# Differential attention: four score maps of a head pair at once, and the long convolution's input made first

## The chip, the cores and the metric

The kernel runs on one core of one Trainium2 chip. The metric is the time of one execution on the device in microseconds (us); three runs of the kernel before gave a median of 2513.32 us. Every number of the trace comes from one profiled execution.

## What is computed

Two transformer blocks stand one behind the other. The first has an mLSTM layer and a latent-attention (MLA) layer, each with a convolutional feed-forward part. The second block has two layers (l = 0, 1), each with four token mixers side by side and an MLP. 256 latent tokens and 256 context tokens run through both; in layer 1 of the second block only the latent tokens are needed at the end. The change is in the second block's mixers, of which two matter here, cut to what is computed:

```python
DIFF_HEADS, DIFF_DQK, CONV_A_K, GROUP_W = 4, 32, 31, 256

def diff_attention(q1, q2, k1, k2, v, lam, lam_init, subln_g):
    scale = DIFF_DQK ** -0.5
    ...
        p1 = jax.nn.softmax(jnp.einsum('bqhd,bkhd->bhqk', qb1, k1).astype(jnp.float32) * scale, axis=-1)
        p2 = jax.nn.softmax(jnp.einsum('bqhd,bkhd->bhqk', qb2, k2).astype(jnp.float32) * scale, axis=-1)
        w = (p1 - lam * p2).astype(v.dtype)
        return jnp.einsum('bhqk,bkhd->bqhd', w, v)
    ...
    o = rms_norm(o, subln_g) * (1.0 - lam_init)

def conformer_conv(a_val, a_gate, conv_w, conv_b, ln_g, ln_b):
    glu = a_val * jax.nn.sigmoid(a_gate)
    y = depthwise_conv(glu, conv_w) + conv_b
    return jax.nn.silu(layer_norm(y, ln_g, ln_b))

    # token_mixers: four mixers, put together and projected
    return jnp.concatenate([y_a, y_b, y_c, y_d], axis=-1) @ w_out
```

So a head has two score maps, each over a contraction of only 32, and the convolution runs over 31 taps of a gated projection. The other two mixers are a spatial gating and a short convolution of 3 taps.

## The kernel before

**Arithmetic.** Every product is made of three matmuls (high x high, high x low, low x high; `mm3`, lines 284 to 286), of operands that `split` (L263, L264) or `weight` (L278, L279) has taken apart: ScalarE rounds the high part, VectorE subtracts it. Weights come in pieces of 512 KB into `raw`.

**Banks.** PSUM has eight banks: four of the pool `pm` (projections and transposes, `mm_ps`), three of `px` (scores, sums, rotations, `ax_ps`), one of `pa`. A tile whose pool is full waits until the oldest tile's readers are done.

**Order.** The kernel is written as one program; a scheduler then sets each engine's order within the limits of data and buffers. What is written earlier goes earlier where both are ready, and `high_priority` lifts the transposes and the weighted values of an item. Each engine runs its own queue in order, so an instruction that waits holds all that stand behind it on that engine.

**The mLSTM's values.** `values_of` (L804) opens four tiles, one for each 128 of a head's 512 value columns, and adds up 16 blocks of the input into each of them. Close to it a head's normalisation runs: sums over tokens by a matmul with ones (L310), eight small steps on VectorE (L845, and L320 to L326, an inverse square root) and a broadcast back by TensorE (L334). The first layer's start (L610 and on) opens seven tiles at once, four `pm` and three `px`.

**The mixers.** `_mixers` (L1363) prepares keys, queries and values, and then runs a loop over the score items. In layer 0 there are two groups, the context (256 queries, 256 keys) and the latent tokens (256 queries, 512 keys); in layer 1 only the latter. A unit is a pair of tiles j, a group and a head g; with two query halves qt that gives 16 items in layer 0 and 8 in layer 1. `probs` makes the two maps of one head in two `px` banks: three matmuls of 32 rows for each, the two strips of 32 rows alternating (L1601), a maximum over each (L1604, VectorE), its negation (L1605), an exponential with its sum (L1608, ScalarE), a reciprocal and a product with 1 and minus lambda (L1611, L1612), and the difference of the two maps (L1613 on ScalarE, L1614 on VectorE). `mix` transposes the result (L1192, `pm`), splits it and multiplies it with the values; `subln` is the head norm (L1650, L1658, L1661).

**The fill.** Beside each item the loop steps a generator `fill`, by the table FS, which makes the remaining projections. In layer 0 it goes: keys and queries of the latent tokens (four pieces), their values, then `gated` (two pieces), then gating and the short convolution, and then the parts of the output projection (`w_oa`). In layer 1 keys, queries and values are made ahead of the loop, so `gated` is the first of the fill. `gated` (L1390) makes the input of the long convolution: two projections, a memset of the tile with its margins (GpSimd), a sigmoid and a product. Once both are there, the loop steps `taps` (L1435), two taps at a time on VectorE (L1444), four such steps per item in layer 0 and three in layer 1. When the taps are through, `conv_norm` follows, with tiles of `px`; what is left of the taps follows behind the loop. The maps of two items stay in the queue (`finish(2)`).

## Time and profile before

| what | value |
|---|---|
| runs | 2507.35, 2513.32, 2513.51 us |
| profiled execution | 2507.25 us |
| its span, first to last instruction | 2505.5 us |
| TensorE busy | 2407.6 us (96%) |
| VectorE busy | 1619.3 us (65%) |
| ScalarE busy | 1109.9 us (44%) |
| mean granted clock of TensorE | 0.976 of full |
| mixers of layer 0 / of layer 1 | about 1558 to 1722 / 2189 to 2290 us |

The names are read so: `px<-a,a 32*128 32x512` is a matmul that writes a tile of `px` from two `a` tiles, with 32 rows of weights, and 512 columns that move. "xcount" joins equal instructions that follow each other; the duration then is that of all of them. The time of a matmul is modelled at its end, so the distance from start to start is the better price. Shares of busy time are means over stages with different limits; the stretches are of more use than the page's totals.

### The profile page before, as it was taken

What the parts mean: (1) busy time and instruction counts of PE and PEld (TensorE: products, weight loads), DVE (VectorE), ACT (ScalarE), POOL (GpSimd) and SP (SyncE); (2) the same over time, 40 slices, a digit from 0 to 9 for tenths busy, and PEclk for the clock granted to TensorE, in tenths of its full rate; (3) what the DMA queues carried; (4) which work ended last, traced back from release to release, by engine and by line L of the source; (5) the groups of instructions that cost most, each with busy time, mean ns of one, the idle gap of its engine ahead of it and who ended that gap; (6) DMA issues with size and microseconds to landing.
All of it is one profiled execution on the core that took longest, in us unless ns stands there. A gap on an engine that the chain in (4) does not pass through costs nothing.

```text
span 2505.5 us, 36625 instructions
## 1 busy us (share of the span) xinstructions
PE 2407.6 (96%) x14362; PEld 2076.6 (83%) x14362; DVE 1619.3 (65%) x2953; ACT 1109.9 (44%) x1879; POOL 11.4 (0%) x20
## 2 busy tenths in 40 slices
PE   7998999999998999999999999989899999998998
PEld 5876888788897878878887999867888888977998
DVE  3867444544567756557676677797865556697665
ACT  4743333422445423235545456554523324465543
POOL 0000000000000000000000000000000000000000
PEclk9999999999999999999998999998899999998999
DMA  8676223433324554556337554222445455233553
GB/s 300 198 233 221 86 85 112 132 93 118 108 78 143 162 158 160 180 165 206 128 119 253 192 179 150 72 84 81 137 157 175 146 160 185 64 91 104 188 183 119
DMA packets 114750, 369.72 MB, mean 148 GB/s; under 512 B 12688, under 2 KB 17040, under 8 KB 114576
## 3 DMA queue, kind: packets, MB, share of 16 engines
q1 hardware_dynamic: 114576, 367.37, 45.0%
q8 instruction: 113, 1.85, 0.3%
q14 instruction: 61, 0.50, 0.1%
HBM read 357.88 MB, written 9.44 MB: 147 GB/s over the span
## 4 chain that ended last, share of the span: by engine, by line
PE 86%; DVE 5%; DMA 3%; ACT 3%; issue 2%; SPq 0%; DVEq 0%; ACTq 0%
PE pm L284 23%; PE pm L285 23%; PE pm L286 22%; PE px L284 4%; PE px L285 4%; PE px L286 4%; DMA raw<-in_ada 2%; DVE a L451 1%; PE px L1601 1%; PE pa L410 1%; PE px L310 1%; DVE wl L279 1%; PE pm L1192 1%; PE px L334 1%; DVE a L279 1%
## 5 line engine op out<-in xcount | busy, mean ns | idle before, releaser
L284 PE MATMUL pm<-a,wh 128*128 128x512 f32 (+1 forms) x2432 | 839.7, 347 | 6.6 <-DVE a L264 3.3
L286 PE MATMUL pm<-a,wl 128*128 128x512 f32 (+1 forms) x2432 | 834.5, 344 | 2.6 <-DVE wl L279 2.6
L285 PE MATMUL pm<-a,wh 128*128 128x512 f32 (+1 forms) x2432 | 836.9, 345 | 0.0
L278 ACT CAST wh<-raw 128x1024 fp32r<-128x1024 f32 (+2 forms) x421 | 420.1, 1002 | 800.1 <-PE pm L285 443.3
L279 DVE TENSOR_TENSOR wl<-raw,wh 128x1024 fp32r<-128x1024 f32 (+2 forms) x421 | 488.2, 1162 | 312.8 <-ACT wh L278 310.5
L284 PEld LDWEIGHTS pm<-a,wh 128*128 128x128 f32 x2432 | 463.3, 191 | 79.7 <-ACT wh L278 11.5
L286 PEld LDWEIGHTS pm<-a,wl 128*128 128x128 f32 x2432 | 463.8, 191 | 56.6 <-DVE wl L279 3.7
L285 PEld LDWEIGHTS pm<-a,wh 128*128 128x128 f32 x2432 | 464.8, 191 | 53.0 <-issue 1.6
L451 DVE SCALAR_TENSOR_TENSOR a<-raw,cs,a 128x1024 f32<-128x1024 f32 x168 | 211.0, 1281 | 91.3 <-DMA raw<-in_ada 89.2
L284 PE MATMUL pm<-a,a 128*128 128x256 f32 (+2 forms) x844 | 245.2, 303 | 16.9 <-ACT a L278 7.6
L285 PE MATMUL pm<-a,a 128*128 128x256 f32 (+2 forms) x844 | 248.8, 297 | 1.5 <-DVE a L279 0.9
L286 PE MATMUL pm<-a,a 128*128 128x256 f32 (+2 forms) x844 | 246.4, 295 | 0.4 <-DVE a L279 0.4
L284 PEld LDWEIGHTS pm<-a,a 128*128 128x128 f32 x844 | 162.8, 197 | 29.1 <-ACT a L278 10.1
L285 PEld LDWEIGHTS pm<-a,a 128*128 128x128 f32 x844 | 166.4, 197 | 4.4 <-DVE a L264 1.2
L286 PEld LDWEIGHTS pm<-a,a 128*128 128x128 f32 x844 | 165.8, 197 | 2.7 <-DVE a L279 0.6
L530 DVE SCALAR_TENSOR_TENSOR a<-pm,mod,a 128x256 f32<-128x256 f32 x188 | 87.3, 480 | 69.5 <-PE pm L286 68.6
L284 PE MATMUL pm<-wh,a 128*128 128x512 f32 (+1 forms) x336 | 128.1, 384 | 3.3 <-ACT a L263 3.3
L285 PE MATMUL pm<-wl,a 128*128 128x512 f32 (+1 forms) x336 | 129.3, 385 | 0.0
L263 ACT CAST a<-t 128x256 fp32r<-128x256 f32 (+2 forms) x173 | 86.1, 505 | 95.4 <-DVE t L1741 49.2
L286 PE MATMUL pm<-wh,a 128*128 128x512 f32 (+1 forms) x336 | 126.0, 383 | 0.0
L284 PE MATMUL px<-a,wh 128*128 128x256 f32 (+1 forms) x364 | 120.3, 331 | 0.0
L285 PE MATMUL px<-a,wh 128*128 128x256 f32 (+1 forms) x364 | 119.7, 330 | 0.0
(309 smaller groups left out, 2940.8 us busy)
## 6 DMA issues: line engine op xcount, KB each, us to landing
raw<-in_ada SPq DMA_DIRECT2D x192, 512.0 KB, 4.3
raw<-in_w_m SPq DMA_DIRECT2D x128, 512.0 KB, 4.2
raw<-in_ffn_in SPq DMA_DIRECT2D x88, 512.0 KB, 4.1
raw<-in_w_qk SPq DMA_DIRECT2D x32, 512.0 KB, 3.6
raw<-in_w_v SPq DMA_DIRECT2D x32, 512.0 KB, 3.5
raw<-in_ffn_oa SPq DMA_DIRECT2D x32, 512.0 KB, 3.6
raw<-in_w_inb SPq DMA_DIRECT2D x28, 512.0 KB, 3.5
raw<-in_w_up SPq DMA_DIRECT2D x16, 512.0 KB, 4.7
```

The costliest lines, as they stand in the source:

```text
L263: self.nc.scalar.copy(hi, src)
L278: nc.scalar.copy(hi, raw)
L279: nc.vector.tensor_sub(lo, raw, hi.bitcast(F32))
L284: mm(out, ah, bh, start=start, stop=False)
L285: mm(out, ah, bl, start=False, stop=False)
L286: mm(out, al, bh, start=False, stop=stop)
L310: self.nc.tensor.matmul(out_ps[:, i * nt + t:i * nt + t + 1], a[:, c0 + t * P:c0 + (t + 1) * P], self.ones[:, 0:1], start=(k == 0), stop=( ...
L334: self.nc.tensor.transpose(ps[:, t * P:(t + 1) * P], col[:, t:t + 1].to_broadcast([P, P]), self.ident)
L410: nc.tensor.matmul(ps[32 * j:32 * j + 32, 0:256], self.cs[:, l // 2, kt, :], raw[:, j, :], start=(kt == 0), stop=(kt == KD - 1), tile_posi ...
L451: nc.vector.scalar_tensor_tensor(s, raw, c, s, op0=ALU.mult, op1=ALU.add)
L530: self.nc.vector.scalar_tensor_tensor(z[:, a:b], ps[:, a:b], gate[:, kt, w:w + 1], z[:, a:b], op0=ALU.mult, op1=ALU.add)
L1192: nc.tensor.transpose(pt[:, s * P:(s + 1) * P], p[:, s * P:(s + 1) * P], K.ident)
```

## The change

- The pools: `pm` has three banks instead of four, `px` four instead of three. Where four or seven tiles are open at once (`values_of`, the mLSTM's start), the fourth of `pm` becomes one of `px`.
- `probs` makes all four maps of a pair of heads in one item: twelve matmuls on the four strips of 32 rows, in turns, into four `px` banks. An item is now a pair of heads and a query half: 8 items in layer 0 and 4 in layer 1. One reciprocal and one product with lambda serve all four maps; two of the four exponentials go to a tile of the pool `a`. `mix` transposes for both heads and opens the `pa` tile just ahead of the products with the values.
- In `fill`, `gated` stands first in both layers.
- The steps per item are set anew (FS; taps by five steps per item in layer 0 and eight in layer 1, the last one being that of the check `next`), and one item stays in the queue instead of two.

```diff
@@ -189,8 +189,8 @@
-        self.pm = E(tc.tile_pool(name="pm", bufs=4, space=bass.MemoryType.PSUM))
-        self.px = E(tc.tile_pool(name="px", bufs=3, space=bass.MemoryType.PSUM))
+        self.pm = E(tc.tile_pool(name="pm", bufs=3, space=bass.MemoryType.PSUM))
+        self.px = E(tc.tile_pool(name="px", bufs=4, space=bass.MemoryType.PSUM))
@@ -610,7 +610,7 @@
-    pss = [K.mm_ps() if f < 4 else K.ax_ps() for f in range(NU)]
+    pss = [K.mm_ps() if f < 3 else K.ax_ps() for f in range(NU)]
@@ -802,7 +802,7 @@
     def values_of(hd):
-        vps = [K.mm_ps() for _ in range(4)]
+        vps = [K.mm_ps() for _ in range(3)] + [K.ax_ps()]
@@ -1557,6 +1557,9 @@
     def fill():
+        for f in range(2):
+            gated(f)
+            yield
         if l == 0:
             for f in range(2):
                 qk_of(kp[f], wk[f], TC, T)
@@ -1565,9 +1568,6 @@
             v_of(vw(), HALVES[1])
-            yield
-        for f in range(2):
-            gated(f)
             yield
@@ -1585,58 +1585,64 @@
-    units = [(j, q0, ns, g) for q0, ns in groups for j in range(2) for g in range(2)]
-
-    def probs(j, q0, ns, g, qt):
+    items = [(j, q0, ns, qt) for q0, ns in groups for j in range(2) for qt in range(2)]
+
+    def probs(j, q0, ns, qt):
...
-        st = K.sp.tile([P, 3, 2], F32, name=K.uid("sd"), tag="sd", bufs=4)
-        p = []
-        ps = [K.ax_ps() for _ in range(2)]
-
-        for n, (u, w) in enumerate(((0, 0), (0, 1), (1, 0))):
-            for i in range(2):
-                rows = slice(64 * g + 32 * i, 64 * g + 32 * i + 32)
-                nc.tensor.matmul(ps[i][:, 0:nk], qp[j][rows, u, sl], kp[j][rows, w, 0:nk],
-                                 start=(n == 0), stop=(n == 2))
-        for i in range(2):
+        st = K.sp.tile([P, 3, 4], F32, name=K.uid("sd"), tag="sd", bufs=4)
+        w = K.a4()
+        ps = [K.ax_ps() for _ in range(4)]
+
+        for n, (u, v) in enumerate(((0, 0), (0, 1), (1, 0))):
+            for i in range(4):
+                rows = slice(32 * i, 32 * i + 32)
+                nc.tensor.matmul(ps[i][:, 0:nk], qp[j][rows, u, sl], kp[j][rows, v, 0:nk],
+                                 start=(n == 0), stop=(n == 2), tile_position=(32 * i, 0))
+        for i in range(4):
             nc.vector.tensor_reduce(st[:, 0, i:i + 1], ps[i][:, 0:nk], axis=AX.X, op=ALU.max)
-        nc.vector.tensor_scalar(st[:, 0], st[:, 0], -scale, None, op0=ALU.mult)
-        for i in range(2):
-            t = K.t2()
-            nc.scalar.activation(t[:, 0:nk], ps[i][:, 0:nk], AF.Exp, bias=st[:, 0, i:i + 1], scale=scale,
+            if i % 2 == 1:
+                nc.vector.tensor_scalar(st[:, 0, i - 1:i + 1], st[:, 0, i - 1:i + 1], -scale, None, op0=ALU.mult)
+        t = []
+        for i in range(4):
+            t.append(w[:, i // 2] if i % 2 == 0 else K.t2())
+            nc.scalar.activation(t[i][:, 0:nk], ps[i][:, 0:nk], AF.Exp, bias=st[:, 0, i:i + 1], scale=scale,
                                  accum_out=st[:, 1, i:i + 1])
-            p.append(t)
         nc.vector.reciprocal(st[:, 2], st[:, 1])
-        nc.vector.tensor_mul(st[:, 2], st[:, 2], lam2)
-        nc.scalar.activation(p[0][:, 0:nk], p[0][:, 0:nk], AF.Copy, scale=st[:, 2, 0:1])
-        nc.vector.scalar_tensor_tensor(p[0][:, 0:nk], p[1][:, 0:nk], st[:, 2, 1:2], p[0][:, 0:nk],
-                                       op0=ALU.mult, op1=ALU.add)
-        return p[0]
+        nc.vector.tensor_tensor(st[:, 2].rearrange("p (g i) -> p g i", g=2), st[:, 2].rearrange("p (g i) -> p g i", g=2),
+                                lam2.unsqueeze(1).to_broadcast([P, 2, 2]), op=ALU.mult)
+        for g in range(2):
+            x = w[:, g, 0:nk]
+            nc.scalar.activation(x, x, AF.Copy, scale=st[:, 2, 2 * g:2 * g + 1])
+            nc.vector.scalar_tensor_tensor(x, t[2 * g + 1][:, 0:nk], st[:, 2, 2 * g + 1:2 * g + 2], x,
+                                           op0=ALU.mult, op1=ALU.add)
+        return w
...
-    FS = ([1] * 8 + [1, 2] * 4, [1] * 4 + [2] * 4)
+    FS = ([2] * 4 + [3] * 4, [2] * 2 + [4] * 2)
     for i, u in enumerate(items):
         queue.append((u, probs(*u)))
         step(filler, FS[l][i])
         if len(glu) == 2 and conv is not None:
-            step(conv, (3,2)[l])
+            step(conv, (4, 7)[l])
...
-        finish(2)
+        finish(1)
```

TensorE, layer 0, the first item of the latent tokens: scores (L1601 before, L1602 now), projections (L284 to L286), the head norm's broadcast (L1661, L1667). Before, a head's two maps of one query half and, 22 rows on, its first map of the other half:

```order
L1661 MATMUL px2328_14623<-cst_89,sq2329_14624 128x128 x2
L1601 MATMUL px2333_14644<-a2189_13789,a2191_13791 128x512
L1601 MATMUL px2334_14645<-a2189_13789,a2191_13791 128x512
L1601 MATMUL px2333_14644<-a2189_13789,a2191_13791 128x512
L1601 MATMUL px2334_14645<-a2189_13789,a2191_13791 128x512
L1601 MATMUL px2333_14644<-a2189_13789,a2191_13791 128x512
L1601 MATMUL px2334_14645<-a2189_13789,a2191_13791 128x512
L285 MATMUL pm2355_14743<-wl2365_14784,a2049_12934 128x512
L286 MATMUL pm2355_14743<-wh2364_14783,a2049_12934 128x512
...
L286 MATMUL pm2356_14744<-wh2367_14801,a2058_12955 128x512
L1601 MATMUL px2344_14713<-a2189_13789,a2191_13791 128x512 x3
L284 MATMUL pa2314_14554<-a2341_14706,a2220_13970 128x256
```

Now:

```order
L1667 MATMUL px2354_14803<-cst_89,sq2355_14804 128x128 x2
L1602 MATMUL px2363_14839<-a2189_13789,a2191_13791 128x512
L1602 MATMUL px2364_14840<-a2189_13789,a2191_13791 128x512
L1602 MATMUL px2363_14839<-a2189_13789,a2191_13791 128x512
L1602 MATMUL px2364_14840<-a2189_13789,a2191_13791 128x512
L1602 MATMUL px2363_14839<-a2189_13789,a2191_13791 128x512
L1602 MATMUL px2364_14840<-a2189_13789,a2191_13791 128x512
L1602 MATMUL px2365_14841<-a2189_13789,a2191_13791 128x512 x3
L284 MATMUL pm2340_14719<-wh2343_14723,a2037_12906 128x512
...
L284 MATMUL pm2341_14720<-wh2346_14741,a2043_12920 128x512
L1602 MATMUL px2366_14842<-a2189_13789,a2191_13791 128x512 x3
L285 MATMUL pm2340_14719<-wl2347_14742,a2043_12920 128x512
```

Three of the four maps are in one piece, the third behind the first two; the fourth stands 15 rows on. Before, the second item's two maps were in separate places too.

TensorE, the mLSTM: values of one head (`pm`, and the fourth tile), sums L310 and broadcast L334. Before:

```order
L285 MATMUL pm624_3899<-wl634_3964,a527_3354 128x512
L310 MATMUL px618_3873<-hm_91,az606_3798 128x1 x4
L286 MATMUL pm624_3899<-wh633_3963,a527_3354 128x512
L284 MATMUL pm625_3900<-wh633_3963,a527_3354 128x512
...
L286 MATMUL pm624_3899<-wh636_3993,a531_3364 128x512
L284 MATMUL pm625_3900<-wh636_3993,a531_3364 128x512
L334 MATMUL px621_3888<-cst_89,rs620_3880 128x128 x4
L285 MATMUL pm625_3900<-wl637_3994,a531_3364 128x512
```

Now:

```order
L284 MATMUL pm624_3899<-wh633_3963,a527_3354 128x512
L285 MATMUL pm624_3899<-wl634_3964,a527_3354 128x512
L286 MATMUL pm624_3899<-wh633_3963,a527_3354 128x512
L310 MATMUL px618_3873<-hm_91,az606_3798 128x1 x4
L334 MATMUL px621_3888<-cst_89,rs620_3880 128x128 x4
L284 MATMUL px625_3900<-wh627_3903,a517_3329 128x512
L285 MATMUL px625_3900<-wl628_3904,a517_3329 128x512
```

The broadcast came 26 rows behind the sums and is now right behind them; the fourth tile's 18 matmuls on the same weights follow it. The same stands in three heads; in the fourth the two are apart as before.

VectorE, layer 0, the first taps (L1442, L1444) with the product that makes their input (L1400), maxima (L1604 before, L1605 now) and weight splits (L279). Before:

```order
L1611 RECIPROCAL sd2278_14343<-sd2278_14343 128x2 [waits Activation_49]
L1612 TENSOR_TENSOR sd2278_14343<-sd2278_14343,lt0_13776 128x2 [waits DVE_49]
L1400 TENSOR_TENSOR a2291_14425<-t2292_14427,pm2283_14363 128x2x256 [waits Activation_49,Pool_49]
L1614 SCALAR_TENSOR_TENSOR t2281_14355<-t2282_14357,sd2278_14343,t2281_14355 128x256 [waits Activation_49]
L1442 TENSOR_SCALAR a2310_14530<-a2291_14425,pv_87 128x512 [waits DVE_49]
L1444 SCALAR_TENSOR_TENSOR a2310_14530<-a2291_14425,pv_87,a2310_14530 128x512 [waits DVE_49] x2
L1604 TENSOR_REDUCE sd2295_14443<-px2297_14445 128x1 [waits PE_49]
L1444 SCALAR_TENSOR_TENSOR a2310_14530<-a2291_14425,pv_87,a2310_14530 128x512 [waits DVE_49]
```

Now:

```order
L279 TENSOR_TENSOR wl2247_14144<-raw2245_14141,wh2246_14143 128x1024 [waits DMAHW2_49,PE_49,Activation_49]
L1400 TENSOR_TENSOR a2238_14104<-t2239_14106,pm2230_14042 128x2x256 [waits PE_49,Activation_49,Pool_49]
L279 TENSOR_TENSOR wl2301_14496<-raw2299_14493,wh2300_14495 128x1024 [waits DMAHW3_49,Activation_49]
L1442 TENSOR_SCALAR a2250_14176<-a2238_14104,pv_87 128x512 [waits DVE_49]
L1444 SCALAR_TENSOR_TENSOR a2250_14176<-a2238_14104,pv_87,a2250_14176 128x512 [waits DVE_49] x5
L279 TENSOR_TENSOR wl2304_14502<-raw2302_14499,wh2303_14501 128x1024 [waits DMAHW4_49,PE_49,Activation_49]
L1444 SCALAR_TENSOR_TENSOR a2250_14176<-a2238_14104,pv_87,a2250_14176 128x512 [waits DVE_49] x4
L1400 TENSOR_TENSOR a2248_14171<-t2249_14173,pm2240_14109 128x2x256 [waits PE_49,Activation_49,Pool_49]
L1605 TENSOR_REDUCE sd2251_14188<-px2255_14192 128x1 [waits PE_49]
L1605 TENSOR_REDUCE sd2251_14188<-px2256_14193 128x1 [waits PE_49]
```

The taps began ahead of the second maximum of the seventh of 16 items, and now begin between the maxima of the second of eight.

## Rows read from the trace of the kernel before

**Rows 1.** The page: busy time by engine; the last chain by line.

```profile
PE 2407.6 (96%) x14362; PEld 2076.6 (83%) x14362; DVE 1619.3 (65%) x2953; ACT 1109.9 (44%) x1879; POOL 11.4 (0%) x20
...
PE pm L284 23%; PE pm L285 23%; PE pm L286 22%; PE px L284 4%; PE px L285 4%; PE px L286 4%; DMA raw<-in_ada 2%; DVE a L451 1%; PE px L1601 1%; PE pa L410 1%; PE px L310 1%; DVE wl L279 1%; PE pm L1192 1%; PE px L334 1%; DVE a L279 1%
```

**Rows 2.** Busy time by stretch, columns as in the first line.

```profile
core 0: us, PE busy (x) PEld busy (x) DVE busy (x) ACT busy (x) POOL busy (x), PEclk, DMA share, GB/s
1558.00:1612.00 54.00, 53.90 (x346) 46.06 (x346) 39.02 (x104) 36.89 (x88) 1.09 (x2) 1.00 0.20 64
1612.00:1710.00 98.00, 89.63 (x417) 70.49 (x416) 92.81 (x206) 47.61 (x88) 0.00 (x0) 0.91 0.22 68
2189.00:2257.00 68.00, 60.10 (x375) 49.88 (x373) 63.62 (x159) 42.70 (x80) 0.00 (x0) 0.93 0.30 90
2257.00:2290.00 33.00, 28.79 (x198) 27.93 (x199) 26.36 (x78) 14.16 (x28) 0.00 (x0) 0.78 0.24 64
1657.00:1663.70 6.70, 6.66 (x19) 5.23 (x20) 6.43 (x18) 3.21 (x8) 0.00 (x0) 0.50 0.15 42
2247.30:2271.20 23.90, 15.10 (x63) 13.24 (x63) 21.51 (x77) 7.41 (x17) 0.00 (x0) 0.50 0.09 23
```

**Rows 3.** TensorE's waits, layer 0 (two lines) and layer 1.

```profile
PE px L1601 <- ACT t L1608: 7.2, 3, 4.6
PE pm L284 <- DVE a L264: 2.6, 1, 2.6
...
PE px L1661 <- DVE sq L1658: 6.5, 2, 6.0
```

**Rows 4.** VectorE's groups, 1558 to 1722: count, busy us, mean ns, idle.

```profile
L1444 DVE SCALAR_TENSOR_TENSOR a<-a,pv,a 128x512 f32<-128x512 f32 x60 | 44.3, 745 | 0.1
L279 DVE TENSOR_TENSOR wl<-raw,wh 128x1024 fp32r<-128x1024 f32 x19 | 23.1, 1219 | 1.0 <-ACT wh L278 1.0
L1604 DVE TENSOR_REDUCE sd<-px 128x1 f32<-128x512 f32 x16 | 10.7, 684 | 1.7 <-PE px L1601 1.7
...
L1611 DVE RECIPROCAL sd<-sd 128x2 f32<-128x2 f32 x16 | 2.6, 162 | 6.6 <-ACT t L1608 6.6
```

**Rows 5.** VectorE's timeline, the first taps: start us, us, instruction, xcount.

```profile
1604.11 1.54 DVE L1444 SCALAR_TENSOR_TENSOR a<-a,pv,a 128x512 f32<-128x512 f32 x2
```

**Rows 6.** TensorE's timeline at two groups of scores; columns as above.

```profile
1630.94 0.96 PE L1601 MATMUL px<-a,a 32*128 32x512 f32 x6
1631.83 0.50 PE L285 MATMUL pm<-wl,a 128*128 128x512 f32 x1
1632.17 0.40 PE L286 MATMUL pm<-wh,a 128*128 128x512 f32 x1
1632.40 0.40 PE L285 MATMUL pm<-wl,a 128*128 128x512 f32 x1
...
1637.07 0.96 PE L1601 MATMUL px<-a,a 32*128 32x512 f32 x3
1637.96 0.39 PE L284 MATMUL pa<-a,a 128*128 128x256 f32 x1
```

**Rows 7.** ScalarE's groups in 1558 to 1722.

```profile
L1608 ACT ACTIVATE t<-px,sd 128x512 f32<-128x512 f32 x16 | 10.8, 684 | 1.6 <-DVE sd L1605 1.5
L1608 ACT ACT_TABLE_LOAD x6 | 7.7, 1283 | 0.1
...
L1608 ACT ACTIVATION_READ_ACCUMULATOR t<-px,sd 128x1 f32 x32 | 6.3, 198 | 0.0
```

**Rows 8.** Timeline of TensorE and VectorE at one mLSTM head's sums.

```profile
568.41 0.95 PE L310 MATMUL px<-hm,az 128*128 128x1 f32 x8
569.22 0.49 PE L286 MATMUL pm<-wh,a 128*128 128x512 f32 x1
...
570.59 0.17 DVE L326 SCALAR_TENSOR_TENSOR rs<-rs 128x4 f32<-128x4 f32 x1
```

**Rows 9.** TensorE's waits in 1030 to 1300, the MLA part.

```profile
PE pm L284 <- DVE a L264: 0.7, 1, 0.7
```

More of the change, by code (lines that the diff above doesn't have):

```diff
@@ L1609, in probs @@
                                  accum_out=st[:, 1, i:i + 1])
-            p.append(t)
         nc.vector.reciprocal(st[:, 2], st[:, 1])
-        nc.vector.tensor_mul(st[:, 2], st[:, 2], lam2)
-        nc.scalar.activation(p[0][:, 0:nk], p[0][:, 0:nk], AF.Copy, scale=st[:, 2, 0:1])
-        nc.vector.scalar_tensor_tensor(p[0][:, 0:nk], p[1][:, 0:nk], st[:, 2, 1:2], p[0][:, 0:nk],
-                                       op0=ALU.mult, op1=ALU.add)
-        return p[0]
-    pso, hl = [None], [None]
@@ L1620, in mix @@
-    def mix(j, q0, ns, g, qt, p):
-        if g == 0 and qt == 0:
-            pso[0] = K.pa.tile([P, 512], F32, name=K.uid("pa"), tag="pa")
-        if qt == 0:
-            if ns == 2:
-                t = K.a4(F32R, (P, 4, TC))
-                hl[0] = t[:, 0:2], t[:, 2:4]
-            else:
-                hl[0] = K.a4(F32R, (P, 4, TC)), K.a4(F32R, (P, 4, TC))
-        hi, lo = hl[0]
-        _transposed(K, p, ns, hi, lo, qt * P)
+        nc.vector.tensor_tensor(st[:, 2].rearrange("p (g i) -> p g i", g=2), st[:, 2].rearrange("p (g i) -> p g i", g=2),
+                                lam2.unsqueeze(1).to_broadcast([P, 2, 2]), op=ALU.mult)
@@ new lines, in probs, with mix @@
+        for g in range(2):
[4 more added lines that the diff above has]
+        return w
+    pso, hl = [None], [None, None]
+    def mix(j, q0, ns, qt, w):
+        if qt == 0:
+            for g in range(2):
+                if ns == 2:
+                    t = K.a4(F32R, (P, 4, TC))
+                    hl[g] = t[:, 0:2], t[:, 2:4]
+                else:
+                    hl[g] = K.a4(F32R, (P, 4, TC)), K.a4(F32R, (P, 4, TC))
+        for g in range(2):
+            _transposed(K, w[:, g], ns, *hl[g], qt * P)
@@ L1631, in mix @@
         if qt == 0:
             return
-        for s in range(ns):
-            K.mm3(pso[0][:, q0:q0 + TC], vz[s][:, 0, 2 * j + g, :], vz[s][:, 1, 2 * j + g, :],
-                  hi[:, s], lo[:, s], g == 0 and s == 0, g == 1 and s == ns - 1)
-        if g == 1:
-            if len(yb) <= j:
-                yb.append(K.a4())
-            nc.scalar.copy(yb[j][:, 0, q0:q0 + TC], pso[0][:, q0:q0 + TC])
+        pso[0] = K.pa.tile([P, 512], F32, name=K.uid("pa"), tag="pa")
+        for g in range(2):
+            hi, lo = hl[g]
+            for s in range(ns):
+                K.mm3(pso[0][:, q0:q0 + TC], vz[s][:, 0, 2 * j + g, :], vz[s][:, 1, 2 * j + g, :],
+                      hi[:, s], lo[:, s], g == 0 and s == 0, g == 1 and s == ns - 1)
@@ L1641, in _mixers @@
+        if len(yb) <= j:
+            yb.append(K.a4())
+        nc.scalar.copy(yb[j][:, 0, q0:q0 + TC], pso[0][:, q0:q0 + TC])
     ybp = {}
@@ L1691, in conv_norm @@
         yield
-    items = [u + (qt,) for u in units for qt in range(2)]
     queue, tails = [], []
@@ L1698, in finish @@
         while len(queue) > n:
-            u, p = queue.pop(0)
+            u, w = queue.pop(0)
             with K.tc.high_priority(60):
-                mix(*u, p)
-            if u[3:] == (1, 1) and u[:2] != (1, TC):
+                mix(*u, w)
+            if u[3] == 1 and u[:2] != (1, TC):
                 tails.append(subln(*u[:2]))
-    FS = ([1] * 8 + [1, 2] * 4, [1] * 4 + [2] * 4)
+    FS = ([2] * 4 + [3] * 4, [2] * 2 + [4] * 2)
     for i, u in enumerate(items):
```

## Prediction

> **What bounds the kernel now.** I read the page first, then the busy time by stretch, then the waits, then single matmuls. The page says that the kernel as a whole is bound by TensorE: 96% of the span; the score matmuls (line L1601) are 1% of the chain that ended last [rows 1]. A change to the score maps can therefore only win where these stages are not held by TensorE alone. There are two such stages, both in the second block: the mixers of layer 0 (1558 to 1722 us) and of layer 1 (2189 to 2290 us). The stretches [rows 2] show a turn inside layer 0. Until 1612 TensorE has no free time (53.90 of 54 us) and VectorE has 15 us of it (39.02 of 54). From 1612 to 1710 it is VectorE that is full (92.81 of 98 us), while TensorE is idle for 8.4 us and its mean clock drops to 0.91. Layer 1 is alike: VectorE 63.62 of 68 us up to 2257, then TensorE at a mean clock of 0.78. The waits [rows 3] name three stalls: scores that wait for the exponentials of an earlier unit (7.2 us, longest 4.6), a projection that waits for a split (2.6), and in layer 1 the sums of squares behind VectorE (6.5, longest 6.0). Inside the stretches after such stalls the granted clock is 0.50, the lower of the two levels (1.2 GHz) [rows 2].
>
> VectorE is full from 1612 on because of the long convolution: 60 taps of 745 ns, 44.3 us, in layer 0 alone [rows 4]. The first of them starts at 1604.11 [rows 5], 46 us into the stage, since its input (`gated`) is made in layer 0 only after five other pieces of the fill.
>
> **The change part by part.**
>
> *Scores on four strips.* Six matmuls on two strips, alternating, take 1630.94 to 1631.83 = 0.89 us; three on a single strip take 1637.07 to 1637.96 = 0.89 too [rows 6]. So two strips already run wholly side by side, and a group costs what three matmuls in a row cost. Two units in one group would save 0.89 us, and some 0.2 us for entering and leaving the group (the matmul behind one, at 1631.83, stands 0.34 us from the next, where 0.23 is usual [rows 6]; I take as much on the other side). But the order of the instructions does not put the four strips together. Of the four latent items of layer 0 none has its twelve matmuls in one piece; they stand as ten groups, where eleven were. In layer 1 two items of four stand whole and one nearly so: seven groups, where twelve were. That is 6 x 1.09 = 6.5 us of TensorE less. The context's maps, of half the columns, go from 10 groups to 12; at half of 0.89 and the same 0.2 that is 1.3 us more. Net 5 us of TensorE, and all but the context's part lies where VectorE, not TensorE, sets the end. I count nothing for it by itself; the bounds are 0 and -5.
>
> The Trainium skill, "TensorEngine Tiling (Array Packing)", Key Properties, says that a change of tiling mode drains TensorE. The trace agrees in size: about 0.1 us on either side [rows 6]. The Trainium skill, "TensorE: Matmul & The Clock Gate", Measured speedup vs the span model, gives 3.07x for four row tiles; by that a full group of four would take some 1.16 us instead of 0.89, an estimate, and as few such groups exist the sum would move by under 1 us.
>
> *Smaller things on VectorE and ScalarE.* Reciprocal and the multiply by lambda go from 24 to 12 each. At 162 ns, the reciprocal's time [rows 4], layer 0 saves 8 + 8 of them, 2.6 us of VectorE; layer 1 saves 4 + 4, 1.3 us. Exponentials stand closer together: three table loads fewer at their line, of 1283 ns each [rows 7], on ScalarE, which is not full (36.89 of 54 us at its most in layer 0 [rows 2]). Nothing counted.
>
> *The convolution's input first, layer 0.* By the order of TensorE, `gated` now stands right behind the first scores, ahead of the other projections. Counted in matmuls at their spacing of before, the first half is there near 1574 instead of just ahead of 1604 [rows 5], and the taps start during the second of the eight items. Between 1574 and 1604 VectorE's free share is 1 - 39.02/54 = 0.28 [rows 2], so 30 x 0.28 = 8 us of taps move out of the full stretch. With the 2.6 us above VectorE has 10.6 us less to do after 1612. VectorE is the bound there, so the stage ends about that much sooner. What is late next is TensorE: it has 89.6 busy us in the 98 from 1612 on, part of it at half clock, so it follows a VectorE that is 10 us sooner if fewer stalls also give back clock. Bounds: as little as 2 us (only the removed operations count, the taps merely push other things on VectorE's queue, weight splits L279 and transposed splits L264, into the early stretch where TensorE is the bound); as much as 17 us (TensorE's whole loss from 1612 to 1710: 8.4 us idle, and 0.09 x 98 = 8.8 us by the clock [rows 2], of which [rows 2] has one piece). I take -10, near the row that bounds it from VectorE's free time.
>
> *Layer 1.* `gated` was first there already, so only the rates change: eight double taps per item instead of three. The taps end with the fourth item and the normalisation follows inside the loop. The stall of 6.0 us before the sums of squares [rows 3] comes from VectorE's queue, where a small chain stands between taps. In the new order some taps still stand there. Saved: 1.3 us of small operations and about half of that stall, 4 us together; bounds 0 and 12 (all of TensorE's free time in both stretches). I take -4.
>
> *One bank from `pm` to `px`.* All of the kernel has three `pm` banks now. In the mLSTM the values of a head need four; the fourth is now `px`. The scheduler then puts 18 of its matmuls behind the others. With that, the sums L310 and the broadcast L334 are adjacent on TensorE in three heads; before, 26 rows of values stood between them. The chain between the two is in the trace: the next matmul after the sums starts at 569.22, and VectorE's eight steps end at 570.59 + 0.17 = 570.76 [rows 8]. So 1.5 us were hidden behind matmuls and stand open now, plus about 0.1 to start: 3 x 1.6 = +4.8 us. Bounds: +3 (a little overlap of the weight loads) and +8.4, if each time a weight split of 1219 ns [rows 4] stands ahead of the chain on VectorE. [...] In the MLA part the transposes share three banks where four were; TensorE waits there for a split only 0.7 us in all [rows 9]; I take +1, bounds 0 and +3. In the ffn and the mlp a tile of `pm` is open for several us of matmuls while its reader takes under 1 us, so the third bank hides that; if that cover fails, about 0.5 us per pair.
>
> *Sum*: -10 - 4 + 4.8 + 1 = -8.2 us. The profiled execution took 2507.25 us, span and 1.75 us around it, so 2499.0. The three runs lie at 2507.35, 2513.32 and 2513.51; the profiled one is at their lower end, and the same step from the median gives 2505.1. I state 2502, between the two.
>
> **The rivals.**
>
> *A: it cancels.* The bank taken from `pm` costs 8 + 3 us and layer 0 gives 6, layer 1 gives 3: +2, about 2509 to 2513. For it: what opens in the mLSTM is certain by the order, and the gain rests on VectorE's free time. Against it: VectorE is full in both places, and the taps do move.
>
> *B: slower, all four banks in one item.* An item takes all of `px`, and the next one's first map waits for the first map's maximum and exponential: 684 ns [rows 4] + 162 for the negation + 684 + 198 to read the sum [rows 7], 1.7 us. Other users of `px` (sums of squares, rotations, the short convolution) have to be let in between. If each of 12 items shows that, 12 x 1.7 = 20 us come on top: -8.2 + 20 = +12, 2519 from the profiled run and up to 2525 from the median. It decides from the point where the fill between two items is shorter than that chain plus what stands ahead of it on VectorE. For it: L1601 waits for exponentials already, with three banks and two taken at a time [rows 3]. Against it: there is fill between items, and a wait of TensorE costs nothing while VectorE is the bound.
>
> *C: it does not do what it says.* The four strips are mostly apart in the order, so the part that gives the change its name yields the 0 that I count; if in addition `gated` only swaps places with other full work, what is left is the removed small operations against the mLSTM's stalls: -3.9 + 5.8 = +2, 2509. For it: the order. Against it: the free 15 us of VectorE ahead of 1612.
>
> *D: layer 0 comes free.* With taps started 30 us sooner VectorE is no longer the bound, the three stalls go, the clock stays at its upper level: -17 - 8 + 5.8 = -19, 2488 to 2494. [...] Against it: 92.81 us of VectorE work do not shrink by more than 10.
>
> **How the numbers follow.** Forecast 0.42, A 0.20, B 0.17, C 0.09, D 0.12. 0.3% (7.5 us) is about what a measurement of this kernel can tell from no change. The forecast lies close to that bound: of its 0.42 I give 0.32 to faster and 0.10 to the same. D is faster. A and C are mostly the same (0.21), with 0.06 slower and 0.02 faster. B is slower. Together faster 0.46, same 0.31, slower 0.23. The range reaches up into B (2520) and takes in the bank's upper bounds with little gain (2507 + 8.4 + 3), and down past D by the rest of layer 1's bound and the scores' 5 us: 2483 to 2520.
>
> **What would show it.** Right: the first tap about 25 us after the stage's start instead of 46, VectorE's share before 1612 up from 39 of 54, the stage of layer 0 about 10 us shorter, L310 to L334 with 1.5 us of TensorE idle in three heads. Rival B shows as a larger wait of the score line for the exponentials; D as a mean clock near 1.0 in layer 0. Wrong: if the taps start early and the stage is no shorter, VectorE was not its bound; if the mLSTM has no new stall, the trace hid a row that the order has.

## The result

The changed kernel takes 2529.61 us (median of four runs, 2523.62 to 2531.24) against 2511.06 for the kernel before: ratio 1.0073, 95% interval 1.0051 to 1.0096. It is slower by about 18 us, where 8 us less was forecast; the time lies above the range (2483 to 2520).

The page after; its lines answer to [rows 1]:

```profile
span 2529.5 us, 36592 instructions
...
PE 2408.9 (95%) x14362; PEld 2079.0 (82%) x14362; DVE 1619.3 (64%) x2929; ACT 1098.1 (43%) x1870; POOL 11.5 (0%) x20
...
PE pm L284 20%; PE pm L285 20%; PE pm L286 20%; PE px L284 4%; PE px L285 4%; PE px L286 4%; DMA raw<-in_ada 3%; DVE a L1444 2%; DVE wl L279 2%; DVE a L451 2%; PE pa L410 1%; PE px L310 1%; DVE a L264 1%; ACT a L263 1%; DVE a L279 1%
```

TensorE is busy for the same time as before (2408.9 and 2407.6 us) in a span that is 24 us longer. So nothing became more work; TensorE waits more. The scores have left the chain, and taps (L1444) and the modulation's matmuls with their weights (L410, in_ada) stand there instead.

Busy time by stretch, columns as in the first line; the first two answer to layer 0 in [rows 2], which starts 22.6 us later by then, the last two to layer 1:

```profile
core 0: us, PE busy (x) PEld busy (x) DVE busy (x) ACT busy (x) POOL busy (x), PEclk, DMA share, GB/s
1580.00:1634.00 54.00, 52.05 (x314) 43.40 (x313) 47.29 (x103) 31.47 (x74) 1.91 (x2) 1.00 0.16 54
1634.00:1732.00 98.00, 86.61 (x421) 68.24 (x419) 80.20 (x182) 50.11 (x99) 0.00 (x0) 0.92 0.23 70
2214.00:2282.00 68.00, 55.51 (x399) 48.41 (x398) 64.00 (x147) 40.42 (x79) 0.00 (x0) 0.98 0.30 94
2282.00:2315.00 33.00, 29.57 (x210) 28.66 (x211) 24.99 (x82) 13.21 (x27) 0.00 (x0) 0.83 0.20 64
```

In layer 0 VectorE did what was forecast: 47.29 of the first 54 us instead of 39.02, and 80.20 of the next 98 instead of 92.81. The first tap (L1442) starts at 1601.79, 21 us into the stage instead of 45. The 12.6 us that VectorE gained are idle time. TensorE does 86.61 us of work in those 98 instead of 89.63. From the first score to the sums of the output norm the layer takes 204.1 us (1580.7 to 1784.8) where it took 200.0 (1558.1 to 1758.1); layer 1 takes 110.6 where it took 112.5. At the first score map the kernel is 22.6 us late already, so nearly all of the loss lies ahead of the part that gives the change its name.

TensorE's waits after, in us, times, longest: of layer 0, of layer 1, and two of 1100 to 1400 us ([rows 3] and [rows 9] are their like before):

```profile
PE px L1656 <- ACT a L1611: 6.5, 2, 5.2
...
PE px L310 <- DVE a L1444: 6.6, 2, 5.4
...
PE pa L410 <- DMA raw<-in_ada: 8.3, 9, 2.3
PE px L419 <- ACT t L416: 3.6, 1, 3.6
```

L1656 makes the sums of the head norm (L1650 before). L419 are transposes of the modulation, which wait for ScalarE's copy; before, L410 waited 2.5 us in this stretch and L419 for nothing that is listed. Another wait is one for a `pm` bank: L365, a step of the convolutions on VectorE, reads a projection's `pm` tile, and no matmul reads what it writes, so a matmul that waits for it waits for that tile's bank. Over the whole execution, after and then before:

```profile
PE pm L284 <- DVE t L365: 9.2, 4, 4.1
...
PE pm L284 <- DVE t L365: 3.9, 2, 2.7
```

With the 0.8 us before for L1116, which reads such a tile too, these waits grow by 4.5 us: 3.4 near 100 us, in the mLSTM's start, the rest near 790 us.

TensorE's timeline after, at five places:

```profile
517.70 0.72 PE L334 MATMUL px<-cst,rs 128*128 128x128 f32 x4 [1.53 <-DVE rs L326]
...
1640.94 0.61 PE L1602 MATMUL px<-a,a 32*128 32x256 f32 x3 [0.94 <-DVE t L1155]
1646.74 1.01 PE L1656 MATMUL px<-ind,a 128*128 128x2 f32 x4 [5.18 <-ACT a L1611]
...
2215.58 0.99 PE L1602 MATMUL px<-a,a 32*128 32x512 f32 x12
2216.51 0.39 PE L285 MATMUL pm<-a,wh 128*128 128x256 f32 x1
...
2281.51 1.02 PE L310 MATMUL px<-hm,a 128*128 128x1 f32 x4 [5.36 <-DVE a L1444]
```

The first is one of the three stalls of the mLSTM heads, as forecast: 1.53 us each. The clock is granted at 0.50 from 518.1 to 521.5, right behind it. The second pair is an item's scores and the head norm's sums; the sums find no `px` bank until an exponential of the item that holds all four. That is what rival B is about, at another place: the score line, which waited 7.2 us for exponentials [rows 3], waits for none now. The third says that four strips do run side by side: twelve matmuls take 0.93 us where six took 0.89 [rows 6].

### The profile page after: what moved, and what is told of

The parts are those of the page before. It is cut to its first block, busy times and chain, and to the rows that moved or that the text cites. A ratio compares the mean times of both kernels' runs of the same rounds, so it can differ in the third digit from the quotient of the medians.

```text
span 2529.5 us, 36592 instructions
## 1 busy us (share of the span) xinstructions
PE 2408.9 (95%) x14362; PEld 2079.0 (82%) x14362; DVE 1619.3 (64%) x2929; ACT 1098.1 (43%) x1870; POOL 11.5 (0%) x20
## 4 chain that ended last, share of the span: by engine, by line
PE 77%; DVE 11%; DMA 4%; ACT 4%; issue 3%; SPq 0%; DVEq 0%; ACTq 0%
PE pm L284 20%; PE pm L285 20%; PE pm L286 20%; PE px L284 4%; PE px L285 4%; PE px L286 4%; DMA raw<-in_ada 3%; DVE a L1444 2%; DVE wl L279 2%; DVE a L451 2%; PE pa L410 1%; PE px L310 1%; DVE a L264 1%; ACT a L263 1%; DVE a L279 1%
## 5 line engine op out<-in xcount | busy, mean ns | idle before, releaser
L284 PE MATMUL pm<-a,wh 128*128 128x512 f32 (+1 forms) x2432 | 840.0, 347 | 10.5 <-DVE t L365 3.4
L286 PE MATMUL pm<-a,wl 128*128 128x512 f32 (+1 forms) x2432 | 835.2, 344 | 4.1 <-DVE wl L279 4.1
L279 DVE TENSOR_TENSOR wl<-raw,wh 128x1024 fp32r<-128x1024 f32 (+2 forms) x421 | 487.9, 1162 | 324.3 <-ACT wh L278 312.1
L284 PEld LDWEIGHTS pm<-a,wh 128*128 128x128 f32 x2432 | 464.0, 192 | 83.9 <-ACT wh L278 10.0
L286 PEld LDWEIGHTS pm<-a,wl 128*128 128x128 f32 x2432 | 464.3, 191 | 57.7 <-DVE wl L279 4.8
L284 PE MATMUL pm<-a,a 128*128 128x256 f32 (+1 forms) x836 | 247.5, 306 | 16.0 <-DVE t L365 5.8
L285 PE MATMUL pm<-a,a 128*128 128x256 f32 (+1 forms) x836 | 249.0, 300 | 1.1 <-DVE a L279 0.9
L286 PE MATMUL pm<-a,a 128*128 128x256 f32 (+1 forms) x836 | 246.9, 298 | 0.5 <-DVE a L279 0.4
L284 PEld LDWEIGHTS pm<-a,a 128*128 128x128 f32 x836 | 164.2, 200 | 29.1 <-ACT a L278 8.0
L286 PEld LDWEIGHTS pm<-a,a 128*128 128x128 f32 x836 | 167.0, 200 | 3.3 <-DVE a L279 1.0
L284 PE MATMUL px<-a,wh 128*128 128x256 f32 (+1 forms) x364 | 120.5, 332 | 0.0
L286 PE MATMUL px<-a,wl 128*128 128x256 f32 (+1 forms) x364 | 119.7, 330 | 0.0
L264 DVE TENSOR_TENSOR a<-t,a 128x256 fp32r<-128x256 f32 (+2 forms) x173 | 93.1, 544 | 28.1 <-ACT a L263 27.3
L285 PE MATMUL pm<-wl,a 128*128 128x512 f32 (+1 forms) x272 | 103.8, 382 | 1.8 <-DVE wl L279 1.8
```

What stands on the lines that cost most here:

```text
L264: self.nc.vector.tensor_sub(lo, src, hi.bitcast(F32))
L279: nc.vector.tensor_sub(lo, raw, hi.bitcast(F32))
L284: mm(out, ah, bh, start=start, stop=False)
L285: mm(out, ah, bl, start=False, stop=False)
L286: mm(out, al, bh, start=False, stop=stop)
```

## The experiments

Each is a copy of the kernel before unless it says otherwise. Ratios are to the kernel before on the same chip, with the 95% interval; 0.001 is 2.5 us.

**The parts one by one.** First the changed kernel again, beside its parts.

> The changed kernel once more, timed beside the others on one chip, so that its parts can be added up against it. Both theories: 1.005 to 1.010 of the kernel before. In its trace three idle pieces of 1.5 us each between the sums (L310) and the broadcast (L334) of three mLSTM heads, and a 5 us piece ahead of the head norm (L1656) in layer 0. What is open: whether the waits of the modulation's matmuls for their weights (L410 for in_ada, 8.3 us in the first profile of it, 2.5 before) come again (they belong to the change) or not (they belong to one execution).

Measured 1.0065 (1.0050 to 1.0080). The waits for in_ada came again: 10.1 us in 1100 to 1400 us, in nine pieces. They belong to the change. The head norm's wait did too: 6.3 us, the longest 4.6.

```diff
-        self.pm = E(tc.tile_pool(name="pm", bufs=4, space=bass.MemoryType.PSUM))
-        self.px = E(tc.tile_pool(name="px", bufs=3, space=bass.MemoryType.PSUM))
+        self.pm = E(tc.tile_pool(name="pm", bufs=3, space=bass.MemoryType.PSUM))
+        self.px = E(tc.tile_pool(name="px", bufs=4, space=bass.MemoryType.PSUM))
-    pss = [K.mm_ps() if f < 4 else K.ax_ps() for f in range(NU)]
+    pss = [K.mm_ps() if f < 3 else K.ax_ps() for f in range(NU)]
-        vps = [K.mm_ps() for _ in range(4)]
+        vps = [K.mm_ps() for _ in range(3)] + [K.ax_ps()]
```

> The kernel before with the pools alone changed (three pm banks, four px; the fourth value tile and the mLSTM start's fourth tile in px); scores, fill and rates as before. Theory banks (most of the loss is the pools): +10 to +15 us, with the three pieces of 1.5 us in the mLSTM heads and more idle time in the MLA part and the second ffn. Theory items (most of the loss is that one item holds all four px banks): +4 to +6, the three heads alone, and layer 0 and 1 of the second block unchanged or a little faster, since a third pair of maps finds a bank sooner.

Measured 1.0068 (1.0052 to 1.0085), 17 us, above the +10 to +15 expected. The pools alone lose what the whole change loses. Counted by equal numbers of the matmuls L284 to L286, the profiled execution is 10.8 us behind that of before at 1000 us, 23.2 at 1360 and 23.3 at the first score map; layer 0 takes 201.3 us. In the changed kernel it is 10.1 at 1100 us and 21.8 at 1360; of these 11.7 us the waits of L410 (5.8 more) and L419 (3.6) make 9.4.

```diff
     def fill():
+        for f in range(2):
+            gated(f)
+            yield
         if l == 0:
...
             v_of(vw(), HALVES[1])
-            yield
-        for f in range(2):
-            gated(f)
             yield
```

> The kernel before with gated put first in the fill, and nothing else. My prediction's step on layer 0: -8 to -10 us, the first tap some 25 us after the stage's start instead of 46. Theory taps-ahead (taps that come early stand ahead of maxima and splits on VectorE and hold up TensorE while TensorE is the bound): 0 to +5, with new idle time of TensorE before 1612 and as many waits for exponentials as before.

Measured 1.0011 (1.0002 to 1.0020), 3 us more instead of 8 to 10 less. Layer 0 takes 204.4 us. The stretch up to 1612 and the next, of `early`:

```profile
1558.00:1612.00 54.00, 47.91 (x285) 39.80 (x284) 44.72 (x100) 32.08 (x70) 1.85 (x2) 0.96 0.16 54
1612.00:1710.00 98.00, 88.61 (x437) 70.26 (x437) 82.72 (x201) 53.58 (x105) 0.00 (x0) 0.92 0.22 68
```

TensorE, which had no free time up to 1612, now has 6 us of it. One stall makes most of them; TensorE's and then VectorE's timeline of `early` around it:

```profile
1605.30 0.62 PE L1601 MATMUL px<-a,a 32*128 32x256 f32 x6
1610.60 0.66 PE L1192 MATMUL pm<-cst,t 128*128 128x128 f32 x2 [4.69 <-DVE sd L1605]
```

```profile
1603.13 0.17 DVE L1605 TENSOR_SCALAR sd<-sd 128x2 f32<-128x2 f32 x1
1603.20 0.75 DVE L1444 SCALAR_TENSOR_TENSOR a<-a,pv,a 128x512 f32<-128x512 f32 x1
...
1605.52 0.17 DVE L1611 RECIPROCAL sd<-sd 128x2 f32<-128x2 f32 x1
1605.60 0.74 DVE L1444 SCALAR_TENSOR_TENSOR a<-a,pv,a 128x512 f32<-128x512 f32 x1
...
1606.91 0.76 DVE L1444 SCALAR_TENSOR_TENSOR a<-a,pv,a 128x512 f32<-128x512 f32 x1
1607.58 0.16 DVE L1612 TENSOR_TENSOR sd<-sd,lt 128x2 f32<-128x2 f32 x1
...
1609.96 0.49 DVE L1614 SCALAR_TENSOR_TENSOR t<-t,sd,t 128x256 f32<-128x256 f32 x1
```

The item's chain (negation, reciprocal, product, difference) takes from 1603.13 to 1610.45 although its steps on VectorE are 0.99 us in sum; taps and splits stand between all of them, and the transposes of the item wait at the end.

The longest stall of `early` in layer 0 is another one: scores that wait for a `px` bank until an exponential has read it, at 1678.36, 23 us behind the last tap. The wait, and ScalarE's timeline ahead of it:

```profile
PE px L1601 <- ACT t L1608: 6.1, 1, 6.1
```

```profile
1674.54 1.28 ACT L1502 ACT_TABLE_LOAD   x1
1675.83 0.38 ACT L1502 ACTIVATE a<-pm 128x256 f32<-128x256 f32 x1
1676.23 1.28 ACT L1608 ACT_TABLE_LOAD   x1
1677.53 0.69 ACT L1608 ACTIVATE t<-px,sd 128x512 f32<-128x512 f32 x1
```

Here no tap stands in the way: half of the 6.1 us are ScalarE's, most of that two table loads.

The fourth copy is the changed kernel on the old pools:

```diff
...
-        ps = [K.ax_ps() for _ in range(4)]
+        ps = [K.ax_ps() for _ in range(3)] + [K.mm_ps()]
```

> The changed kernel on the pools of the kernel before (four pm, three px): the fourth map of an item takes a pm bank; values and mLSTM start as before. Theory banks: -2 to -8 us against the kernel before, as the loss is gone with the swap. Theory items: +5 to +12, since an item now holds all three px banks and one of pm, and the head norm's and the convolution's norm's tiles wait for its exponentials as in the changed kernel.

Measured 1.0024 (1.0013 to 1.0034), 6 us, at the lower end of theory items: without the pools' change two thirds of the loss are gone, but what remains of the change costs and does not gain. The two do not add up: 17 us for the pools and 6 for the rest are 23, the whole 16.5.

**Which part of the pools.** Only the fourth value tile in `px`, on four and three banks:

> The kernel before, with its four pm and three px banks; only the fourth value tile of a head is taken from px. It splits the loss of the pools (banks: +17 us) in two. Theory heads (the loss is where the fourth value tile makes the broadcast L334 follow the sums L310): the three idle pieces of 1.5 us again, and +8 to +15 in all. Theory scarce (the loss is that every other part has three pm banks): 0 to +5, for the three pieces of 1.5 us and the half clock that may follow one of them, less what the first head gains; nothing behind 740 us.

Measured 1.0014 (1.0005 to 1.0024), 3.5 us. The three stalls are there, 4.6 us in sum, and the loss is the one that theory scarce expects. Next, a `pm` bank held by a tile of one column:

```diff
+        hold = K.mm_ps()
+        nc.vector.memset(hold[:, 0:1], 0.0)
         gen1 = K.ada_v(1)
...
+        nc.vector.tensor_add(sink, hold[:, 0:1], z[3][:, 1, T - 1:T])
         h, mod = h2, mod2
```

> The kernel before, but one pm bank is held from the end of the mLSTM's output projection to the start of the second block's mixers by a tile of one column that is written there and read at the end (one memset and one addition on VectorE more). px keeps three banks. Theory scarce: the MLA part and the second ffn lose what they lose in banks, +8 to +12 us between 1100 and 1400 us, with waits of L410 for in_ada and the 3.6 us of L419. Theory heads: 0 to +2.

Measured 1.0048 (1.0033 to 1.0063), 12 us, with both waits that theory scarce names (L410 8.0 us in 1100 to 1400 us, L419 3.6). 3.5 + 12 is 15.5 of the 17. Held through the MLA part alone, by a tile that a copy writes ahead of it and an addition reads behind it:

> As pm3_mid, but the pm bank is held only through the MLA part (some 1100 to 1310 us) and is free again for the second ffn. pm3_mid lost 12 us, by its trace about 5 in MLA, 4 at 1310 to 1360 and the rest before 1100 and behind 1540. Theory MLA: 1.0015 to 1.003. Theory ffn (the third bank costs where gate and up tiles are open in pairs): 1.000 to 1.001.

Measured 1.0060 (1.0039 to 1.0082), 15 us, above what both theories expect: holding the bank through the MLA part alone costs no less than through MLA and ffn together, so the parts do not add up here either. TensorE's waits of `pm3_mlaonly` in 1100 to 1400 us (first two), its timeline at the worst place, and the same wait and two of these groups before:

```profile
PE pa L410 <- DMA raw<-in_ada: 19.8, 12, 4.7
PE px L284 <- ACT a L278: 1.2, 1, 1.2
```

```profile
1166.89 1.08 PE L410 MATMUL pa<-raw,cs 128*32 128x256 f32 x8 [4.69 <-DMA raw<-in_ada]
...
1169.37 1.08 PE L410 MATMUL pa<-raw,cs 128*32 128x256 f32 x8
1172.64 1.08 PE L410 MATMUL pa<-raw,cs 128*32 128x256 f32 x8 [2.18 <-DMA raw<-in_ada]
1175.30 1.08 PE L410 MATMUL pa<-raw,cs 128*32 128x256 f32 x8 [1.58 <-DMA raw<-in_ada]
1178.83 1.08 PE L410 MATMUL pa<-raw,cs 128*32 128x256 f32 x8 [2.46 <-DMA raw<-in_ada]
1181.31 1.08 PE L410 MATMUL pa<-raw,cs 128*32 128x256 f32 x8 [1.40 <-DMA raw<-in_ada]
```

```profile
PE pa L410 <- DMA raw<-in_ada: 2.5, 4, 0.8
...
1171.85 0.64 PE L410 MATMUL pa<-raw,cs 128*32 128x256 f32 x8
1175.12 0.64 PE L410 MATMUL pa<-raw,cs 128*32 128x256 f32 x8
```

No new wait for a bank is listed in this stretch. The modulation's matmuls, which in the kernel before stand some 3 us apart between projections, stand here one behind the other, and five of the six groups of eight wait for weights (four matmuls use one piece of 512 KB). They take 1.08 us where they took 0.64, at a granted clock of 0.50 from 1168 to 1182 us. From 1100 to 1400 us the same waits are 2.5 us in the kernel before and 8.3 in the changed one.

To see whether that place is the whole cause, the modulation was written out whole ahead of the MLA part, with and without the held bank:

```diff
+        K.finish(gen2)
         h, (g2, b2) = {}, lg(2)
         _mla(K, h1, z, mod1, _Ln(K, z, g2, b2, K.affine(mod1, 4, 3, g2, b2), ALPHA, h, LAT, LAT))
```

> The kernel before, with the second block's modulation (its matmuls L410 on the weights in_ada) written out whole ahead of the MLA part instead of in pieces beside it. It is the partner of pm3_fin; against the kernel before 0.998 to 1.006 by both theories, since work that was spread stands together.

> pm3_mid (one pm bank held through MLA and ffn, +12 us) with the modulation whole ahead of the MLA part as in fin. Theory order (three banks make the scheduler pull the modulation's matmuls ahead of where their weights land, and the waits for these weights are the loss): at most +4 us over fin, and hardly a wait of L410 in 1110 to 1400 us that fin has not. Theory scarce (TensorE waits for a bank's reader): +8 to +12 over fin again, as projections and transposes still share three banks.

Measured 1.0112 (1.0097 to 1.0127), outside what was expected, and 1.0158 (1.0141 to 1.0175). The held bank costs 12 us again, though L410 waits alike in both (14.4 and 13.9 us in 700 to 1440 us). In the same stretch, without the held bank (two lines) and with it:

```profile
PE pm L284 <- DVE t L365: 2.7, 2, 1.6
...
PE pm L284 <- DVE t L1116: 2.2, 1, 2.2
...
PE pm L284 <- DVE t L365: 9.5, 3, 4.1
```

L365 and L1116 read `pm` tiles of the ffn, so these are waits for a bank, and they grow by 4.6 us. The 12 us are what theory scarce expects, and its reason is seen for 4.6 of them; theory order falls as a full account. Which wait opens with three banks differs from copy to copy.

**Layer 0.** The convolution's input early, taps held back to the seventh item:

> The kernel before with gated first in the fill, as in early, but in layer 0 the taps are held back until the seventh item, where they started before. Theory taps-ahead (early taps stand ahead of maxima and splits on VectorE): back to the kernel before, 0.999 to 1.000. Theory order (what costs is that the keys and queries of the latent tokens come later): as early, 1.001 to 1.002, with TensorE idle again ahead of 1612 us.

Measured 1.0047 (1.0032 to 1.0062), the reverse of what taps-ahead expects. Up to 1612 TensorE has no stall (53.95 of 54 us), but then VectorE is full as in the kernel before, and the stage is longer still, 209.4 us. With the score chain lifted in priority, on `early` and on the kernel before:

```diff
-        queue.append((u, probs(*u)))
+        with K.tc.high_priority(60):
+            pr = probs(*u)
+        queue.append((u, pr))
```

> early (gated first on the kernel before; 1.0011) with the steps of probs lifted in priority, so that the scheduler puts maxima, negation, reciprocal, product and difference ahead of ready taps. In early, TensorE stood 4.7 us ahead of transposes (L1192) while on VectorE taps of 750 ns stood between the 0.16 us steps of that chain. Theory chain-behind-taps: that wait goes, layer 0 takes 4 to 8 us less than in early, 0.997 to 0.999 of the kernel before. Theory bound (layer 0 is held by the sum of VectorE's work, whichever comes first): as early, 1.000 to 1.002.

> The kernel before with the steps of probs lifted in priority and nothing else, the partner of early_prio. Theory chain-behind-taps: a gain here too, 0.998 to 1.000, since in the kernel before the chain stands among taps from 1604 us on. Theory bound: 1.000 to 1.002.

Measured 1.0045 (1.0030 to 1.0061) and 1.0017 (1.0006 to 1.0028). Priority for the chain does not win the time back; layer 0 of `early_prio` takes 213.8 us and has waits of 5.7 and 5.5 us in sum ahead of transposes.

**The four-map items.** On the old pools, with `gated` in its old place:

> The changed kernel on the pools of before (as strips43), with gated back behind the latent projections in layer 0, and the taps at eight steps per item in both layers, so that they still end within the loop: of the change only the items of four maps remain. Theory strips are good (early costs 0.11%, strips43 0.24%, so the items cost at most the difference): 1.000 to 1.002. Theory items: 1.003 or more, as the head norm and the convolution's norm still wait for banks behind four exponentials.

Measured 1.0004 (0.9994 to 1.0013): level. Against `strips43` the old place of `gated`, with more taps per item, is 5 us better. Its layer 1 takes 118.5 us instead of 112.5, with this wait:

```profile
PE px L310 <- DVE a L1444: 9.6, 2, 7.1
```

> strips43_late (items of four maps on the pools of before, gated late; 1.0004) with the taps of layer 1 at their old rate, three steps an item, so that the rest of them and the convolution's norm come behind the loop. In strips43_late layer 0 took some 4.7 us less than before and layer 1 3.7 more, with 7.1 us of TensorE's idle time ahead of the sums L310 of the convolution's norm that wait for the last tap. Theory norm-in-the-loop (those 7 us come from the norm's place): 0.998 to 0.999. Theory items (layer 1 is slower by the items themselves): 1.000 to 1.001.

> strips43_late with the taps at eight steps in layer 1 too, but the convolution's norm of layer 1 written behind the loop. Theory norm-in-the-loop: as mix43 or better, 0.997 to 0.999, as taps are through early and TensorE does not stand ahead of them. Theory items: 1.000 to 1.001.

Measured 1.0011 (0.9998 to 1.0024) and 1.0006 (0.9996 to 1.0017): moving the convolution's norm out of the loop gains nothing, and layer 1 takes 120.1 us in both. That theory fell. It left the items of layer 1 themselves, on three `px` banks and one of `pm` (on the four `px` banks of the changed kernel layer 1 took 110.6 us). So in the last copy layer 0 alone has items of four maps:

```diff
+    if l == 0:
+        items = [(j, q0, ns, qt) for q0, ns in groups for j in range(2) for qt in range(2)]
...
+            ps = [K.ax_ps() for _ in range(3)] + [K.mm_ps()]
...
+    FS = ([2] * 4 + [3] * 4, [1] * 4 + [2] * 4)
...
+            step(conv, (7, 2)[l])
...
+        finish(1 + l)
```

> Pools and first fill order of the kernel before; layer 0 with items of four maps (fourth map in a pm bank) as in strips43_late, layer 1 with items of two maps, its rates and its queue as before. Theory place (layer 0 gains 4.7 us from the four-map items as long as the convolution's input is not moved, layer 1 loses by them): -3 to -5 us, 0.998 to 0.999. Theory items: nothing to gain, 1.000 to 1.001, and the gain seen in layer 0 was chance of one order.

Measured 0.9978 (0.9968 to 0.9988), 2506.28 us (median of 11 runs), faster than both kernels. Its stretches of layer 0:

```profile
1558.00:1612.00 54.00, 51.85 (x341) 44.38 (x340) 38.73 (x105) 36.63 (x94) 2.93 (x4) 1.00 0.16 54
1612.00:1710.00 98.00, 92.47 (x449) 73.29 (x447) 95.04 (x201) 50.10 (x88) 0.00 (x0) 0.95 0.23 73
```

From 1612 on TensorE does 92.47 us of work instead of 89.63 at a clock of 0.95 instead of 0.91, with VectorE as full as it was; its layer 0 starts 3.8 us later, so the stretches are shifted by as much. The head norm waits for exponentials here too, 5.3 us in layer 0. Layer 1 takes 112.4 us, as before. One caution on the lengths of layer 0: the same order of TensorE in `strips43_late`, `mix43` and `mix43_norm` took 197.0, 199.8 and 201.6 us in one execution each, and `vpx`, which leaves the mixers' code as it was, 204.4. Lengths of a stage within 5 us are no evidence by themselves; the ratios are.

## Why the prediction was wrong

- *What bounds the layers.* That VectorE is full from 1612 on was read rightly, and the conclusion from it was not: "VectorE is the bound there, so the stage ends about that much sooner". The taps came early and VectorE got its 10 us (12.6), and the stage was not shorter, which the prediction itself names as the sign that VectorE was not its bound. The term -10 measures +3 in `early`. What TensorE waits for there is an item's chain of small steps through three engines: 4.7 us while its steps on VectorE stand behind taps, and 6.1 us (7.2 before) for an exponential that ScalarE comes to late, with no tap left. Free time on VectorE does not shorten the second. With the taps held back it is slower still (1.0047). That the chain is the whole cause is not shown: priority for it did not help.
- *Scores on four strips.* Rightly counted at nothing: few items stand whole, the 5 us of TensorE can't be seen in its busy time, and four strips run at once. The Trainium skill, "TensorE: Matmul & The Clock Gate", Measured speedup vs the span model, has 3.07x for four row tiles; here four strips take 0.93 us where one takes 0.89 [rows 6], 3.8x. The measurement decides; the sum is the same by either.
- *Layer 1.* -4 forecast, -1.9 in the profiled pair, which is less than one and the same order of layer 0 differs by from execution to execution. The stall that was to be halved (6.0 us, [rows 3]; it stood ahead of the head norm's broadcast, L1661, and not of sums of squares) is gone, and another of its size has opened: L310, the sums of the convolution's norm, waits 5.4 us for the last taps.
- *One bank from pm to px.* The step that failed most. The three stalls of the heads are 1.53 us each, 4.6 us, as the +4.8 said, and `vpx` as a whole 3.5. The failed words are "in the MLA part the transposes share three banks where four were; TensorE waits there for a split only 0.7 us in all; I take +1, bounds 0 and +3". It was priced as if the order stayed and only waits for banks could be added. The order did not stay, and a `pm` bank less from the MLA part on costs 12 us (`pm3_mid`), through MLA alone 15 (`pm3_mlaonly`), by its trace mostly in waits for weights and, in the changed kernel, for the modulation's transposes. Waits for banks grew as well: by 3.4 us in the mLSTM's start, for which the prediction has nothing, and by some 0.5 us at each of two places of the ffn, the price that it names ("if that cover fails, about 0.5 us per pair") and leaves out of the sum. The rows of that order could be read beforehand; I read the mLSTM's and the mixers' and not the modulation's.
- *The clock.* The sum has no term for it behind the three stalls. Behind the first of them the clock fell to 0.50 for 3.4 us. In the trace of before it fell already at 2247.3 us [rows 2], 1.4 us behind a wait of 1.27 us and ahead of the stall of 6.0.
- *The rivals.* By its own sign B did not come: the score line waits for no exponential. What B names, one item that holds all banks, is real at the head norm (5.18 us at one place, 6.5 us in layer 0) but is not the cause of the loss: `banks` has no item of four maps and loses as much. It is seen in `strips43` too (2.2 us), where the four maps hold three `px` banks and one of `pm`, and in `hybrid`, which is faster than the kernel before. A and C price the bank's loss at 5.8 to 11 us and miss it; D's sign, a clock near 1.0, did not come (0.92 from 1634 on).
- *The range* ended at 2520 since the bounds of the bank's cost (+3 to +8.4 and 0 to +3) were bounds of the waits that I had thought of.

What stays open: how the loss with three `pm` banks, which stays at 12 to 17 us, divides between waits for a bank and the new order (the waits differ from copy to copy). No run has the held tile's two operations without a held bank, nor the order of three banks on four, so what any other order would cost is not known. Open too is why priority for the score chain makes layer 0 longer.

## What to carry to other kernels

Where a scheduler sets the order, a change of a pool's size is a change of the whole program: compare the order in every stage that uses the pool, above all where instructions that wait for DMAs have moved, and time the pool's change alone before what it was made for. A full engine is not the bound of a stage while another one waits for a chain through it: ask how long the chain takes from end to end, not how much work there is. An idea that is made of several edits is worth the taking apart: of this one the four-map items in layer 0 alone gain 0.2%, and the rest takes 0.9% back.

## What the runs showed that I had not expected

A bank that holds one unused column from the MLA part's start to its end costs 15 us (0.60%), with no new wait for a bank listed in that stretch of the trace. One and the same order of TensorE's instructions took 197.0 to 201.6 us in layer 0 in three executions.
